# A 512-column product for both parts of the tokens in the input products of four FFNs

## Chip, core and metric

The kernel runs on one core of one Trainium2 chip. The metric is the device time of one execution in microseconds (us). Besides the timed runs there is one execution that was recorded by the hardware profiler; every duration below is from that recording.

The engines are called as the profile calls them: PE (TensorE; PEld is its weight load), DVE (VectorE), ACT (ScalarE), POOL (GpSimd) and SP (SyncE, which here only issues DMAs). Each engine works through its own instructions in program order and waits on semaphores for the others.

## What is computed

A trunk of two layers for 256 tokens of 1024 channels. Each layer has three sublayers, each with a residual and a layer norm: half an FFN (SwiGLU), a mixer (S5 in layer 0, gMLP in layer 1), half an FFN. So there are four FFNs, and each computes

```python
def _swiglu(x, w_in, w_out):
    gate, up = jnp.split(x @ w_in, 2, axis=-1)   # w_in: 1024 x 5632
    return (jax.nn.silu(gate) * up) @ w_out      # w_out: 2816 x 1024

h = _layernorm(DN_ALPHA * h + 0.5 * _swiglu(h, w_in, w_out), ln_g, ln_b)
```

All arrays are float32.

## The kernel before

**Two parts.** PE multiplies in the type float32r. To keep precision, each operand is split into a first part `hi` (the value cast to float32r, on ACT) and a second part `lo` (the value minus `hi`, on DVE). A product is the sum of three: hi x hi, hi x lo and lo x hi.

**The weights** come as a stream of 1 MiB blocks, in the order of their use (class `Stream`). SP issues the load of a block into one of 3 `raw` buffers (line 60); a split makes `hi` on ACT (line 82) and `lo` on DVE (line 83), into a ring of 5 pairs. The load of the block three places on waits until the DVE half of a split has freed its `raw` buffer. `ws.tick()` stands at fixed places in the program: it splits the next block if the ring has room, and then takes one piece of background work from a list. In the first FFN that list is the preparation of the S5 parameters (`prepare_s5`): some DVE work, some copies on ACT, and a long queue of small operations on POOL (lines 592 and 596), which begins with `turn_a`: four transposes on PE, four copies on ACT (lines 648 and 651), and then an exponential on POOL. POOL also makes the reciprocal root `rstd` for every layer norm (lines 203 and 204), behind what stands in its queue.

**The tokens** stand transposed in `xt`, as [128 channels, 2 halves of the tokens, 2 parts, 8 k, 128 tokens].

**An FFN** works in 11 chunks of 256 gate and 256 up columns. The first chunks are computed with tokens on the partitions (`start_in` in the first FFN, chunk 0; `step_in` in the others, chunks 0 and 1). All others, 10 in the first FFN and 9 in each of the three others, go through `chunk_in`: for m (two halves of 128 columns), for g (gate, up), for k (8 steps of 128 channels), the three products of `mm3t` with 256 columns, one for each token, into a PSUM tile [128, 2 g, 256 tokens]. Then `act_t`: silu of the gate from PSUM on ACT (line 368), times the up half from PSUM on DVE (line 369), a cast for the first part on ACT (370) and a difference for the second on DVE (371), into `gt`. Two chunks later `step_out` multiplies `gt` with the rows of `w_out` (512 columns, lines 183 to 185, tile `acc`). `close` does the last three chunks' output products and the norm, and it begins the next sublayer's transposes of `h`.

**Buffers.** PSUM pool `mm` has 4 buffers of one bank; the input products' tiles (`ips`) and the transposes' tiles (`tps`, `aps`) take turns in them. `sgg` (silu and product) has 2 buffers, in which the first FFN's two column tiles of chunk 0 stand before chunk 1 begins; the transposes `tps` of `finish_g`, which come after the products of chunk 1's first half, are the last to read those. `gt` has 7 buffers, and POOL's tables `tb` take turns in them.

Of the kernel before, what the change touches and what calls it, by code (L numbers as in the profile page):

```python
# [9 lines left out]
F32 = mybir.dt.float32  # L10
# [3 lines left out]
ALU = mybir.AluOpType  # L14
# [27 lines left out]
class Stream:  # L42
    """Weights in the order of their use: 1 MiB blocks that are loaded ahead and split into two float32r parts."""
# [41 lines left out]
    def split_pieces(self, n):  # L85
        """Begins to split a block; the returned function splits one of n pieces of it."""
        nc = self.nc
        raw, hi, lo = self.next_block()

        def piece(p):  # L90
            s = slice(p * SUB // n, (p + 1) * SUB // n)
            nc.scalar.copy(hi[:, s], raw[:, s])  # L92
            nc.vector.tensor_tensor(lo[:, s], raw[:, s], hi[:, s].bitcast(F32), op=ALU.subtract)

        return piece

    def split_slowly(self):
        """Splits a block but for the second parts, which the returned two pieces of work make."""
        nc = self.nc
        raw, hi, lo = self.next_block()  # L100
        nc.scalar.copy(hi, raw)

        def rest(p):
            s = slice(p, p + SUB // 2)
            nc.vector.tensor_tensor(lo[:, s], raw[:, s], hi[:, s].bitcast(F32), op=ALU.subtract)
            if p and self.n_loaded < len(self.specs):
                self.load()

        return [lambda p=p: rest(p) for p in (0, SUB // 2)]
# [6 lines left out]
    def tick(self, n=1, pieces=1, eng=None):  # L116
        """Splits up to n more blocks, as far as the ring has room; then a piece of the work that nothing waits for."""
        while n and self.n_split < len(self.specs) and self.n_split - self.n_done < N_SPLIT:
            self.split(pieces, eng)
            self.fill()  # L120
            n -= 1
        if self.background:
            self.background.pop(0)()
# [13 lines left out]
def hybrid(ctx: ExitStack, tc: tile.TileContext, a: dict, out: bass.AP, subs=SUBS):  # L137
# [26 lines left out]
    def transpose_split(src, hi, lo, n, perm=False):  # L164
        """Transposes n 128-column blocks of src [128 tokens, n*128] into hi/lo [128, n, 128]; perm: tokens ordered
        by (token % 4, token // 4)."""
        ps = mm_p.tile([P, 512], F32, tag="mm", name="tps")
        for j in range(n):
            nc.tensor.transpose(ps[:, j * P:(j + 1) * P], src[:, j * P:(j + 1) * P], ident)
        v = ps[:, :n * P].rearrange("p (n t) -> p n t", n=n)  # L170
        if perm:
            v = v.rearrange("p n (k t) -> p n t k", t=T)
            hi, lo = (x.rearrange("p n (t k) -> p n t k", t=T) for x in (hi, lo))
        nc.scalar.copy(hi, v)
        nc.vector.tensor_tensor(lo, v, hi.bitcast(F32), op=ALU.subtract)
# [11 lines left out]
    def mm3t(ps, wh, wl, k, start, stop):  # L187
        """The product with the columns of w on the partitions, for all tokens."""
# [3 lines left out]
        nc.tensor.matmul(ps, wl, xh, start=False, stop=stop)  # L192

# [21 lines left out]
    def layernorm(t, acc, gb, hscale, eps):  # L215
        """h <- LN(hscale*h + acc)"""
# [10 lines left out]
    def add_cols(w, col, width):  # L227
        """Two blocks with the columns [col, col + width) of w: [128, 4 k, width] each."""
# [6 lines left out]
    def add_rows(w, row):  # L235
        """One block with 256 rows of w: [128, 2 k, 1024]."""
# [16 lines left out]
    def close(li, si, acc, blocks, mm, gb, hscale, eps, last):  # L253
        """The last blocks of a sublayer's output product, then its norm: half 0, then half 1 beside the next sublayer."""
# [20 lines left out]
    def plan_ffn(li, fi, fine):  # L275
# [3 lines left out]
        def add_in(c):  # L279
            """Two blocks: [128, 4 k, (gate, up), 256]."""  # L280
# [26 lines left out]
    def ffn(ids, li, si, first, last):  # L307
# [39 lines left out]
        def chunk_in(c):  # L347
            """A chunk for all tokens, the chunk's columns on the partitions."""
            for m in range(2):
                ps = mm_p.tile([P, 2, SEQ], F32, tag="mm", name="ips")  # L350
                for g in range(2):
                    for k in range(KD):
                        wh, wl = ws.get(ids["in"][c][k // 4])
                        s = slice(512 * (k % 4) + FC * g + P * m, 512 * (k % 4) + FC * g + P * m + P)
                        mm3t(ps[:, g], wh[:, s], wl[:, s], k, k == 0, k == KD - 1)
                    if (m, g) == (1, 1):
                        done(ids["in"][c])
                    if g:
                        act_t(c, m, ps)
# [4 lines left out]
        def act_t(c, m, ps):  # L364
            sgg = g_p.tile([P, 2, SEQ], F32, tag="sgg", name="sgg")
            sg, g = sgg[:, 0], sgg[:, 1]
            x = new_gt(c, m)
            nc.scalar.activation(sg, ps[:, 0], AF.Silu)  # L368
            nc.vector.tensor_tensor(g, ps[:, 1], sg, op=ALU.mult)  # L369
            nc.scalar.copy(x[:, 0], g)  # L370
            nc.vector.tensor_tensor(x[:, 1], g, x[:, 0].bitcast(F32), op=ALU.subtract)  # L371

        def start_in():
            """The first chunk of the kernel, both halves of the tokens after each piece of its weights."""
# [65 lines left out]
    def close_mixer(ids, li, si, operand, gb, hscale, eps, last):  # L440
        """The output product of a mixer; operand(k, t): the two parts of 128 of its columns, transposed."""
# [18 lines left out]
    def load_gmlp(pool):  # L460
        """The parameters of the gMLP mixer but for its two projections; W_s masked and transposed."""
# [24 lines left out]
    def gmlp(plan, par, pool, li, si, first, last):  # L486
# [20 lines left out]
        def step_u(hd):  # L507
            """u of one head, its channels on the partitions."""
# [19 lines left out]
        def spatial(hd):  # L528
            """The token mixing of two heads and the gate, in place of u."""
# [35 lines left out]
    def load_column(pool, src, name):  # L565
        """[1024] as [128, 8], channel 128 j + p at [p, j]."""
# [10 lines left out]
    def prepare_s5(sm, qp, dram):  # L577
        """Parameters of the S5 mixer in the layouts of its use, as pieces of work for the time of the first FFN.

        State s of pair q is state s % 64 of group 2 q + s // 64. Four tokens make one step:  # L580
        S' = lam^4 S + sum over t of lam^(3-t) B u[4k+t], y[4k+3] = Re(C S'), and for t < 3
        y[4k+t] = Re(C lam^(t+1) S) + sum over i <= t of K(t-i) u[4k+i], K(d) = Re(C lam^d B).
        With lam^4 = m e^(i phi), e^(-i phi k) S is a scan with real factors m.
        """
# [28 lines left out]
        def exp(x, name):  # L613
            """e^x: 2^k of the nearest integer k to x / ln 2, in two factors, times a polynomial in the rest."""
# [101 lines left out]
        def spread():  # L716
            """The factors of B with (token of the step, state % 32) on the partitions."""
# [6 lines left out]
        def seed():  # L724
            """The square of a unit number, brought back to length 1."""
# [15 lines left out]
        def grow(x, level, z):  # L741
            """e^(i phi k) for 2^level <= k < 2^(level+1) from those below; x: (cos, sin), [128, q, k]."""
# [34 lines left out]
        # lam^(3-t) B, zero where a state and a channel are of different groups of a pair; its  # L777
        # rows: (token of the step, channel)
# [30 lines left out]
        # the same B with the states on the partitions, for K  # L809
# [16 lines left out]
        # C lam^d with the states on the partitions, zero where the groups differ  # L826
# [16 lines left out]
        def c_lam(d, j, part, e):  # L843
            """C lam^d from C lam^(d-1), the real part or the imaginary part's negative."""
# [65 lines left out]
    def s5(plan, res, qp, li, si, first, last):  # L910
# [29 lines left out]
        def turn_u():  # L940
            """u of 4 x 128 channels: [channel, (token of the step, step)], half of the steps."""
# [20 lines left out]
        def turned(dst, src, ct):  # L962
            """src times the cosines and src times the sines; src: (real, imaginary)."""
# [76 lines left out]
        def finish(n):  # L1040
            """2 z = y (1 + tanh(x / 2)), its tokens in their order, in two parts."""
# [159 lines left out]
```

## Time and profile before

| | us |
|---|---|
| median of 3 runs | 1044.12 |
| lowest, highest | 1043.42, 1046.18 |
| the profiled execution: its own time, the span from the first instruction to the last | 1044.0 |
| PE busy in it | 964.5 (92%) |
| DVE, ACT, POOL busy | 651.6, 413.1, 302.0 |

The stages as the trace shows them: the first FFN to about 256 us, the S5 mixer to about 385, the second FFN to about 577, the third to about 768, the gMLP mixer to about 855, the fourth FFN to the end.

How to read the lines that follow. A timeline row has: start in us, length in us, engine, source line, operation, what it writes and what it reads, shapes, count (neighbours are merged into one row), and in brackets how long its engine had stood idle and which instruction ended that. A row of groups has: line, engine, operation, count, busy us in all and the mean of one in ns, idle time before. Products overlap in PE's pipeline, so the length of one is a latency, and the pace is the distance between two starts.

### The profile page before, as it was taken

The page shows a single profiled execution, that of the slowest core. Times are in us where ns is not written, and L with a number is a line of the kernel's source. Part 1 is how long each engine was busy: PE and PEld are TensorE (multiplying, and loading weights), DVE is VectorE, ACT ScalarE, POOL GpSimd, SP SyncE. Part 2 cuts the span into 40 slices and gives each one's busy share as a digit, 9 for nine tenths or more (in the row PEclk, how much of TensorE's full clock was granted, in tenths as well). Part 3 has the DMA queues.
Part 4 walks back from the last instruction along what each step waited for, and adds up shares of the span by engine and source line. Part 5 has one row for each costly group of instructions (what it writes and reads, how often), then busy time and mean ns, then how long its engine had stood idle before and what let it go on. Part 6 is the DMA issues. An engine that isn't in the chain of part 4 may idle for free.

```text
span 1044.0 us, 16750 instructions
## 1 busy us (share of the span) xinstructions
PE 964.5 (92%) x6988; PEld 871.9 (84%) x6988; DVE 651.6 (62%) x726; ACT 413.1 (40%) x467; POOL 302.0 (29%) x461
## 2 busy tenths in 40 slices
PE   7999974577988889999999999999999999999996
PEld 6999963475877678999999799999978979999995
DVE  5659834588489776654536764545388785545444
ACT  5462333232143244453533363534335535443430
POOL 1589999998156421000000400000031030000001
PEclk9999996697998999999999999999999999999999
DMA  9977553385466434746455667465544565546431
GB/s 282 205 216 236 184 150 126 130 298 180 169 216 239 149 127 161 258 147 216 164 200 178 223 209 258 149 215 170 193 162 174 190 209 194 204 160 221 142 122 41
DMA packets 146124, 194.86 MB, mean 187 GB/s; under 512 B 26992, under 2 KB 117184, under 8 KB 146048
## 3 DMA queue, kind: packets, MB, share of 16 engines
q1 hardware_dynamic: 142304, 180.81, 52.7%
q0 software_dynamic: 3456, 12.45, 3.5%
q8 instruction: 55, 0.90, 0.3%
q10 hardware_dynamic: 288, 0.52, 0.1%
q14 instruction: 21, 0.17, 0.0%
HBM read 183.94 MB, written 9.83 MB: 186 GB/s over the span
## 4 chain that ended last, share of the span: by engine, by line
PE 59%; POOL 20%; DVE 10%; issue 4%; ACT 3%; DMA 2%; SPq 1%; POOLq 0%; DVEq 0%; ACTq 0%
PE ips L192 10%; PE ips L191 10%; PE ips L190 10%; PE acc L183 5%; PE acc L184 5%; PE acc L185 5%; POOL rot L972 3%; DVE lo L83 2%; POOL fac L592 2%; POOL t L592 2%; PE ips L185 2%; POOL cl L592 2%; PE ips L183 2%; PE ips L184 2%; POOL tb L592 2%
## 5 line engine op out<-in xcount | busy, mean ns | idle before, releaser
L83 DVE TENSOR_TENSOR lo<-raw,hi 128x2048 fp32r<-128x2048 f32 (+1 forms) x146 | 333.9, 2318 | 85.2 <-ACT hi L82 82.5
L190 PE MATMUL ips<-xt,hi 128*128 128x256 f32 x1184 | 335.3, 283 | 0.0
L191 PE MATMUL ips<-xt,hi 128*128 128x256 f32 x1184 | 335.0, 283 | 0.0
L192 PE MATMUL ips<-xt,lo 128*128 128x256 f32 x1184 | 335.0, 283 | 0.0
L82 ACT CAST hi<-raw 128x2048 fp32r<-128x2048 f32 (+1 forms) x156 | 275.1, 1797 | 62.7 <-PE acc L185 22.1
L190 PEld LDWEIGHTS ips<-xt,hi 128*128 128x128 f32 x1184 | 227.1, 192 | 1.4
L191 PEld LDWEIGHTS ips<-xt,hi 128*128 128x128 f32 x1184 | 227.2, 192 | 1.4
L192 PEld LDWEIGHTS ips<-xt,lo 128*128 128x128 f32 x1184 | 227.1, 192 | 0.0
L203 POOL TENSOR_SCALAR rstd<-mv 128x1 f32<-128x1 f32 x14 | 10.3, 733 | 586.3 <-DVE mv L224 564.4
L183 PE MATMUL acc<-hi,gt 128*128 128x512 f32 x352 | 141.9, 403 | 29.3 <-ACT hi L82 29.3
L184 PE MATMUL acc<-lo,gt 128*128 128x512 f32 x352 | 141.2, 401 | 4.6 <-DVE lo L83 4.6
L185 PE MATMUL acc<-hi,gt 128*128 128x512 f32 x352 | 140.2, 398 | 0.0
L369 DVE TENSOR_TENSOR sgg<-ips,sgg 128x256 f32<-128x256 f32 x74 | 31.1, 420 | 158.8 <-ACT sgg L368 158.8
L368 ACT ACTIVATE sgg<-ips 128x256 f32<-128x256 f32 x74 | 28.4, 383 | 207.9 <-PE ips L192 204.0
L183 PEld LDWEIGHTS acc<-hi,gt 128*128 128x128 f32 x352 | 68.5, 195 | 43.2 <-ACT hi L82 29.7
L370 ACT CAST gt<-sgg 128x256 fp32r<-128x256 f32 x74 | 30.1, 406 | 149.9 <-DVE sgg L369 100.9
L184 PEld LDWEIGHTS acc<-lo,gt 128*128 128x128 f32 x352 | 68.3, 194 | 18.8 <-DVE lo L83 5.9
L185 PEld LDWEIGHTS acc<-hi,gt 128*128 128x128 f32 x352 | 68.1, 193 | 14.7
L371 DVE TENSOR_TENSOR gt<-sgg,gt 128x256 fp32r<-128x256 f32 x74 | 34.1, 461 | 69.9 <-ACT gt L370 69.9
L183 PE MATMUL ips<-hi,xt 128*128 128x512 f32 x112 | 45.9, 410 | 1.7 <-ACT hi L92 1.0
L972 POOL TENSOR_TENSOR rot<-rot 128x256 f32<-128x256 f32 x32 | 35.8, 1137 | 40.1 <-DVE rot L966 39.8
L185 PE MATMUL ips<-hi,xt 128*128 128x512 f32 x112 | 45.0, 402 | 0.1
(250 smaller groups left out, 1275.9 us busy)
## 6 DMA issues: line engine op xcount, KB each, us to landing
raw<-in_ffn_w_in SPq DMA_DIRECT2D x172, 512.0 KB, 5.5
raw<-in_ffn_w_out SPq DMA_DIRECT2D x44, 1024.0 KB, 5.1
raw<-in_g_w_in SPq DMA_DIRECT2D x8, 1024.0 KB, 5.9
rows<-w SPq DMA_DIRECT2D x8, 512.0 KB, 6.0
raw<-in_s_w_in SPq DMA_DIRECT2D x4, 1024.0 KB, 5.5
raw<-in_s_w_glu SPq DMA_DIRECT2D x4, 1024.0 KB, 5.0
w<-rows SPq DMA_DIRECT2D x8, 512.0 KB, 5.8
tc<-tc SPq DMA_DIRECT2D x8, 512.0 KB, 5.1
```

Source lines behind the costliest of these rows:

```text
L82: nc.scalar.copy(hi[:, s], raw[:, s])
L83: eng[p % len(eng)].tensor_tensor(lo[:, s], raw[:, s], hi[:, s].bitcast(F32), op=ALU.subtract)
L183: nc.tensor.matmul(ps, xh, wh, start=start, stop=False)
L184: nc.tensor.matmul(ps, xh, wl, start=False, stop=False)
L185: nc.tensor.matmul(ps, xl, wh, start=False, stop=stop)
L190: nc.tensor.matmul(ps, wh, xh, start=start, stop=False)
L191: nc.tensor.matmul(ps, wh, xl, start=False, stop=False)
L192: nc.tensor.matmul(ps, wl, xh, start=False, stop=stop)
L369: nc.vector.tensor_tensor(g, ps[:, 1], sg, op=ALU.mult)
L371: nc.vector.tensor_tensor(x[:, 1], g, x[:, 0].bitcast(F32), op=ALU.subtract)
L592: e.tensor_tensor(o, x, y, op=op)
L972: G.tensor_tensor(dst[:, j], x, z, op=ops[j])
```

## The change

The three products of one k become two. `mm3t` stays for the gMLP mixer; `chunk_in` calls a new `mm2t`:

```diff
+    def mm2t(ps, wh, wl, k):
+        both = ps.rearrange("p j (t c) -> p j t c", t=2)
+        nc.tensor.matmul(both, wh, xt[:, :, :, k].rearrange("p t j c -> p j t c"), start=k == 0, stop=False)
+        nc.tensor.matmul(ps[:, 0], wl, xt[:, :, 0, k], start=False, stop=k == KD - 1)
...
         def chunk_in(c):
             for m in range(2):
-                ps = mm_p.tile([P, 2, SEQ], F32, tag="mm", name="ips")
+                ps = [mm_p.tile([P, 2, SEQ], F32, tag="mm", name="ips") for _ in range(2)]
+                sgg = g_p.tile([P, 2, SEQ], F32, tag="sgg", name="sgg")
                 for g in range(2):
                     for k in range(KD):
...
-                        mm3t(ps[:, g], wh[:, s], wl[:, s], k, k == 0, k == KD - 1)
+                        mm2t(ps[g], wh[:, s], wl[:, s], k)
                     if (m, g) == (1, 1):
                         done(ids["in"][c])
-                    if g:
-                        act_t(c, m, ps)
+                    nc.scalar.copy(sgg[:, g], ps[g][:, 1])
+                    nc.vector.tensor_tensor(sgg[:, g], sgg[:, g], ps[g][:, 0], op=ALU.add)
+                    if g == 0:
+                        nc.scalar.activation(sgg[:, 0], sgg[:, 0], AF.Silu)
+                    else:
+                        act_t(c, m, sgg)
                     if (m, g) == (0, 1):
                         finish_g()
                     ws.tick()
 
-        def act_t(c, m, ps):
-            sgg = g_p.tile([P, 2, SEQ], F32, tag="sgg", name="sgg")
-            sg, g = sgg[:, 0], sgg[:, 1]
-            x = new_gt(c, m)
-            nc.scalar.activation(sg, ps[:, 0], AF.Silu)
-            nc.vector.tensor_tensor(g, ps[:, 1], sg, op=ALU.mult)
+        def act_t(c, m, sgg):
+            x, g = new_gt(c, m), sgg[:, 1]
+            nc.vector.tensor_tensor(g, g, sgg[:, 0], op=ALU.mult)
             nc.scalar.copy(x[:, 0], g)
             nc.vector.tensor_tensor(x[:, 1], g, x[:, 0].bitcast(F32), op=ALU.subtract)
```

The first part of the weights is multiplied with both parts of the tokens in one product of 512 columns, whose two halves land in the two halves of a PSUM bank; the product of the second part of the weights adds to the first half. Gate and up have a bank each. ACT copies the second half to `sgg`, DVE adds the first half to it. Silu and the product with it then read `sgg`, not PSUM. The rest of the diff removes comments. The lines after the change are numbered higher by 7 in `step_in` and the functions before it, and by 9 from `start_in` on.

PE, the beginning of `chunk_in(1)` in the first FFN (`hi_237` and `lo_238` are the parts of a block of `w_in`, `hi_244` and `lo_245` those of the next): before,

```order
L190 MATMUL ips<-xt,hi_237 128x256
L191 MATMUL ips<-xt,hi_237 128x256
L192 MATMUL ips<-xt,lo_238 128x256
L190 MATMUL ips<-xt,hi_244 128x256
L191 MATMUL ips<-xt,hi_244 128x256
L192 MATMUL ips<-xt,lo_245 128x256
```

and after the change:

```order
L198 MATMUL ips<-xt,hi_237 128x512
L199 MATMUL ips<-xt,lo_238 128x256
L198 MATMUL ips<-xt,hi_244 128x512
L199 MATMUL ips<-xt,lo_245 128x256
```

Each pair of products with the first part of the weights has become one of 512 columns.

ACT in the same place, from the silu of the first FFN's two column tiles to the copies of `turn_a` (`ar`), behind which POOL's queue stands (`hi` from `raw` is a split): before,

```order
L331 ACTIVATE sgg<-ips 128x256 x2
L82 CAST hi_287<-raw_234 128x2048
L368 ACTIVATE sgg<-ips 128x256
L370 CAST gt<-sgg 128x256
L325 CAST gt<-tps 128x128 x4
L82 CAST hi_346<-raw_241 128x2048
L82 CAST hi_385<-raw_248 128x2048
L648 COPY ar<-aps 128x32
```

and after:

```order
L338 ACTIVATE sgg<-ips 128x256 x2
L366 COPY sgg<-ips 128x256
L369 ACTIVATE sgg<-sgg 128x256
L82 CAST hi_284<-raw_234 128x2048
L366 COPY sgg<-ips 128x256
L379 CAST gt<-sgg 128x256
L332 CAST gt<-tps 128x128 x4
L82 CAST hi_335<-raw_241 128x2048
L366 COPY sgg<-ips 128x256
L369 ACTIVATE sgg<-sgg 128x256
L82 CAST hi_371<-raw_248 128x2048
L657 COPY ar<-aps 128x32
```

The copy and the silu of a gate half now stand ahead of the split from `raw_234`, and those of the next gate half between the two splits that stood together. The first copy writes the `sgg` buffer that the transposes `tps` read last.

DVE in the same place (`lo` from `raw` is the DVE half of a split, `cz` a buffer of the S5 preparation): before,

```order
L332 TENSOR_TENSOR sgg<-ips,sgg 128x256 x2
L83 TENSOR_TENSOR lo_288<-raw_234,hi_287 128x2048
L829 MEMSET cz_294 128x1024
L369 TENSOR_TENSOR sgg<-ips,sgg 128x256
L371 TENSOR_TENSOR gt<-sgg,gt 128x256
L326 TENSOR_TENSOR gt<-tps,gt 128x128 x4
L83 TENSOR_TENSOR lo_347<-raw_241,hi_346 128x2048
```

and after:

```order
L339 TENSOR_TENSOR sgg<-ips,sgg 128x256 x2
L367 TENSOR_TENSOR sgg<-sgg,ips 128x256
L83 TENSOR_TENSOR lo_285<-raw_234,hi_284 128x2048
L838 MEMSET cz_291 128x1024
L367 TENSOR_TENSOR sgg<-sgg,ips 128x256
L378 TENSOR_TENSOR sgg<-sgg 128x256
L380 TENSOR_TENSOR gt<-sgg,gt 128x256
L333 TENSOR_TENSOR gt<-tps,gt 128x128 x4
L83 TENSOR_TENSOR lo_336<-raw_241,hi_335 128x2048
```

An addition stands ahead of the DVE half of the first split and another behind the memset, and the product (`L378`) has both its operands in `sgg`.

## Prediction

> **What bounds the kernel now.** I read the page's slices and its chain first.
>
> ```profile
> PE   7999974577988889999999999999999999999996
> ...
> POOL 1589999998156421000000400000031030000001
> ...
> PE 59%; POOL 20%; DVE 10%; issue 4%; ACT 3%; DMA 2%; SPq 1%; POOLq 0%; DVEq 0%; ACTq 0%
> ```
>
> TensorE (PE) is full from the sixteenth slice on, and POOL is full from the third to the tenth. The chain that ended last is 59% PE and 20% POOL. So the kernel has two regimes, and the table by stretches separates them (columns: stretch, length, busy time and count of PE, PEld, DVE, ACT, POOL, then clock, DMA share, GB/s).
>
> ```profile
> 36.80:250.90 214.10, 173.86 (x1371) 159.23 (x1369) 142.99 (x137) 76.03 (x80) 195.66 (x354) 0.90 0.64 198
> ...
> 592.00:768.00 176.00, 175.71 (x1192) 162.84 (x1191) 93.51 (x89) 76.38 (x83) 4.90 (x7) 1.00 0.61 205
> ```
>
> In an FFN such as the third (second row) PE is busy 175.7 of 176.0 us while DVE and ACT are about half idle: there a shorter PE stream is a shorter kernel. In the first FFN (first row) POOL, which prepares the S5 parameters, is busy 195.7 of 214.1 us while PE has 40 us idle. The timeline shows that this stage ends with POOL:
>
> ```profile
> 36.76 0.35 POOL L596 TENSOR_SCALAR ldt<-ldt 128x32 f32<-128x32 f32 x1 [18.86 <-ACT dg L651]
> ...
> 70.06 0.59 POOL L592 TENSOR_TENSOR mag<-mag,ee 128x32 f32<-128x32 f32 x2 [1.17 <-DVE ee L636]
> ...
> 251.97 0.97 POOL L204 TENSOR_TENSOR rstd<-rstd,mhalf 128x1 f32<-128x1 f32 x1
> ...
> 252.98 5.58 DVE L213 SCALAR_TENSOR_TENSOR h<-r,rstd,bet 128x512 f32<-128x512 f32 x2 [0.47 <-POOL rstd L204]
> ...
> 255.86 1.11 PE L169 MATMUL tps<-ident,h 128*128 128x128 f32 x4 [5.46 <-DVE h L213]
> ```
>
> POOL starts when ACT has copied the parameters (36.76), then stands in one queue to the `rstd` of the first norm at 251.97, which DVE waits for and PE waits for in turn. Only one wait on another engine in that queue matters, 1.17 us at 70. A PE that is faster in the first FFN therefore gains nothing there, and a POOL that starts later ends later.
>
> **PE: the term that gains.** Start to start in the second FFN:
>
> ```profile
> 559.82 0.28 PE L190 MATMUL ips<-xt,hi 128*128 128x256 f32 x1
> ...
> 562.58 0.28 PE L192 MATMUL ips<-xt,lo 128*128 128x256 f32 x1
> ...
> 564.09 0.39 PE L183 MATMUL acc<-hi,gt 128*128 128x512 f32 x1
> ...
> 570.88 0.39 PE L183 MATMUL acc<-hi,gt 128*128 128x512 f32 x1
> ...
> L190 PE MATMUL ips<-xt,hi 128*128 128x256 f32 x1184 | 335.3, 283 | 0.0
> ```
>
> From the first to the second row are 23 steps of 256 columns: 2.76 / 23 = 120.0 ns. From the third to the fourth are 30 steps of 512 columns: 6.79 / 30 = 226.3 ns. (The 283 ns of the group is one product's latency; they overlap, so the pace counts.) Twice 120.0 is 13.7 ns more than 226.3: a product pays that much whatever its width. Per k the change replaces three narrow products (360.0 ns) by a wide and a narrow one (346.3 ns), one weight load fewer. The 1184 k-steps are 32 in each of 37 chunks; 27 chunks lie in FFNs 2 to 4, which PE bounds: 27 x 32 x 13.7 ns = **11.8 us gained**. No row shows a wide product that reads its columns in four runs; the bounds are no saving (0) and 11.8, and I take 11.8, because 256 columns in two runs and 512 in one leave the same 13.7. The other 10 chunks (4.4 us) are in the first FFN and count nothing.
>
> The Trainium skill, "TensorE: Matmul & The Clock Gate", section "Back-to-back issue gap", gives a product N / 2.4 + 2.5 ns; by it the saving would be about 2.5 ns per k and 2.2 us in all. The trace disagrees: 120.0 and 226.3 where the page has 109.2 and 215.8.
>
> **ACT and DVE in FFNs 2 to 4.** Each half-chunk gains two copies (ACT) and two additions (DVE). The nearest rows are `L368` (0.38 us) and `L369` (0.42 us), both quoted below with 256 columns from PSUM; four of each per chunk of about 17 us are 1.6 us, on engines about half idle. The gate's pair is done while PE works on the up half, so it is hidden. The up half's addition is not hidden in a sublayer's last chunk: the weight splits queue behind it on DVE, and the norm behind them.
>
> ```profile
> 566.09 4.49 DVE L83 TENSOR_TENSOR lo<-raw,hi 128x2048 fp32r<-128x2048 f32 x2 [1.40 <-ACT hi L82]
> 570.50 0.68 DVE L221 SCALAR_TENSOR_TENSOR r<-h,acc 128x512 f32<-128x512 f32 x1
> ...
> 576.78 0.39 PE L185 MATMUL acc<-hi,gt 128*128 128x512 f32 x1
> 578.31 0.66 PE L169 MATMUL tps<-ident,h 128*128 128x128 f32 x4 [1.14 <-DVE h L213]
> ```
>
> The norm follows the splits without a break, and PE waits for its `h` (1.14 us). So the added 0.42 and a hand-over, 0.45 us, are late at PE after the second and third FFN: **0.9 us lost**.
>
> PSUM: each gate and each up tile now takes a buffer, so a product waits for the addition of the tile four before it (one chunk, 17 us) instead of two chunks. In FFNs 2 to 4 that addition comes within about 3 us, behind three splits. Nothing is lost.
>
> **The first FFN: the term that loses.** The rows of its start, ACT, then DVE:
>
> ```profile
> 24.05 1.90 ACT L82 CAST hi<-raw 128x2048 fp32r<-128x2048 f32 x1
> ...
> 29.74 0.38 ACT L368 ACTIVATE sgg<-ips 128x256 f32<-128x256 f32 x1 [3.79 <-PE tps L322]
> ...
> 30.61 0.41 ACT L370 CAST gt<-sgg 128x256 fp32r<-128x256 f32 x1 [0.49 <-DVE sgg L369]
> ...
> 32.69 3.73 ACT L82 CAST hi<-raw 128x2048 fp32r<-128x2048 f32 x2
> ...
> 36.53 0.22 ACT L651 COPY dg<-aps 128x16 f32<-128x16 f32 x1
> ...
> 28.46 0.91 DVE L829 MEMSET cz<- 128x1024 f32 x1 [0.16 <-issue]
> ...
> 30.15 0.42 DVE L369 TENSOR_TENSOR sgg<-ips,sgg 128x256 f32<-128x256 f32 x1 [0.78 <-ACT sgg L368]
> ...
> 34.63 4.51 DVE L83 TENSOR_TENSOR lo<-raw,hi 128x2048 fp32r<-128x2048 f32 x2 [1.51 <-ACT hi L82]
> ```
>
> Of chunk 1's first `sgg` the row at 29.74 shows the wait: its buffer is still read by the transposes `tps` behind both column tiles. Now that wait sits on the gate's copy, which stands **ahead** of the split at 24.05. ACT is in order, so that split is held, and with it all that follows. From the same durations: copy, addition, silu 29.7 to 30.95; split 1.9, to 32.85; its DVE half 2.25, to 35.1; the memset, to 36.0; addition and product, to 36.9; the cast and the two transposed tiles, 2.08 as from 30.61 to 32.69, to 39.0; split 1.9 and its DVE half 2.3, to 43.2; addition and silu of the next gate, to 44.05; split 1.9, to 45.9; then the copies that POOL waits for, 46.2. Before, the two splits at 32.69 ran without a break and the copies ended at 36.75. POOL starts **9.5 us later**; of the 1.17 us at 70 it gets about 0.9 back: 8.6. (The DVE step that it waits for there is behind splits whose loads SP issues when an earlier split frees a buffer; those start 7 to 10 us later too, and by the same steps DVE is there at about 78, when POOL is.) PE, held by these splits and by PSUM, is some 5 us late after two chunks, and DVE gets 1.6 us more per chunk (four additions). Both have room:
>
> ```profile
> 167.83 0.41 ACT L370 CAST gt<-sgg 128x256 fp32r<-128x256 f32 x1 [24.80 <-POOL s5t L592]
> ...
> 199.26 0.40 ACT L370 CAST gt<-sgg 128x256 fp32r<-128x256 f32 x1 [14.67 <-POOL s5t L592]
> ```
>
> Twice ACT, and DVE and PE behind it, stand 25 and 15 us for buffers that POOL holds.
>
> The other cost is that POOL stalls beside DVE:
>
> ```profile
> 83.18 0.41 DVE L369 TENSOR_TENSOR sgg<-ips,sgg 128x256 f32<-128x256 f32 x1
> ...
> 84.06 0.43 DVE L371 TENSOR_TENSOR gt<-sgg,gt 128x256 fp32r<-128x256 f32 x1 [0.47 <-ACT gt L370]
> ...
> 89.49 2.33 DVE L83 TENSOR_TENSOR lo<-raw,hi 128x2048 fp32r<-128x2048 f32 x1 [1.34 <-ACT hi L82]
> ...
> 83.33 0.25 POOL L592 TENSOR_TENSOR t<-lr,fac 128x32 f32<-128x32 f32 x1
> ...
> 84.20 0.40 POOL L592 TENSOR_TENSOR t<-lr,fac 128x32 f32<-128x32 f32 x1
> ...
> 89.75 2.18 POOL L592 TENSOR_TENSOR t<-lr,fac 128x32 f32<-128x32 f32 x1
> ```
>
> The same POOL operation takes 0.25 us beside a DVE operation that reads PSUM, 0.40 beside a short one with two SBUF operands, and 2.18 beside a long one. The 40 added additions read PSUM: no cost. The 20 products read PSUM before and two SBUF operands now: 0 to 0.43 us each, I take the row's 0.15: 20 x 0.15 = 3.0 us (ends 0 and 8.6). At the stage's end the longer DVE queue (some 5 us for two chunks) falls into the time in which DVE waits for `rstd`: 0 to 2, I take 0. First FFN: 8.6 + 3.0 = **11.6 us lost**.
>
> **Sum.** The profiled execution's own time is its span, 1044.0, with nothing shown outside it; the runs' median is 1044.12. 1044.0 - 11.8 + 0.9 + 11.6 = 1044.7 us: PE's gain in three FFNs is given back in the first.
>
> **Rivals.**
> - Slower, by POOL's stalls: each of the 20 products holds POOL for its whole 0.43 us, 8.6 instead of 3.0, and the DVE queue adds its 2 at the end: 1044.7 + 5.6 + 2 = 1052.3. The place is the stretch up to 251; it decides above 0.28 us each, where 2.6 us more than my 3.0 pass the bound of 0.3%. For it: 2.18 beside the long split. Against it: 0.40 beside the short operation. The Trainium skill, "SBUF — State Buffer", section "SBUF: two separate sides", has this rule: a DVE operation with two SBUF inputs takes the port pair shared with GpSimd exclusively, for the whole instruction. The trace agrees for the split, not for the short one. Chance 0.22.
> - Faster: the late start doesn't reach the end of the first FFN, because POOL has room that I don't see. Fully absorbed it is 1044.7 - 11.6 = 1033.1; half, 1038.9. For it: POOL's busy time contains stalls beside DVE, and these may fall elsewhere. Against it: it never waited over 1.3 us after 36.8. Chance 0.22.
> - The wide product brings no pace, or the four runs cost their own 13.7 ns: 1044.7 + 11.8 = 1056.5. By the page's gap it would be 1054.3. Against it: the rows of PE. Chance 0.08.
>
> **How the numbers follow.** What I forecast, no change, has 0.48. A measurement here tells about 0.3% (3.1 us) from nothing: same is 1041 to 1047, 0.48; slower 0.22 + 0.08 = 0.30; faster 0.22. The range, 1035 to 1053, takes in most of both sides and leaves out a full absorption and the pace that fails. The likeliest case alone has 1041 to 1047.
>
> **What would show it.** In the changed profile: wide products 226 and narrow 120 ns apart, FFNs 2 to 4 shorter by about 11 us together; POOL's first `ldt` at about 46 instead of 36.8; `rstd` of the first norm at about 263; ACT idle from 24 to 29.7 before the gate's copy. If `rstd` comes by 255, the second rival is right; if the start is 46 and `rstd` past 268, the first; if the wide step is over 235 ns, the third.

## The result, and the profile after

The changed kernel takes 1056.55 us (median of 4 runs, 1055.74 to 1057.87) against 1045.15 us (1043.42 to 1047.8): ratio 1.0111, interval 1.0091 to 1.0132. It is **slower by 11.4 us**, outside the predicted range. The profiled execution's span is 1054.5 us, 10.5 above the span before; the run that it belongs to took 1056.29 us.

From the page of the changed kernel, the slices of POOL and the chain that ended last:

```profile
POOL 1289999998426613000000400000021030000001
...
PE 56%; POOL 20%; DVE 13%; issue 5%; ACT 3%; DMA 2%; SPq 1%; POOLq 0%; DVEq 0%; ACTq 0%
```

POOL's second slice has fallen from 5 to 2 tenths and its eleventh has risen from 1 to 4, so it starts later and ends later, and DVE has 13% of the chain instead of 10%. Where the 10.5 us are is read from the table by stretches, one row for each sublayer but the gMLP's, whose 73.4 us did not change. A sublayer ends here where the first transposes `tps` of the next begin; the gMLP mixer's end by that mark is 843.31, while the norm of the second half of its tokens, about 855, comes 12 us later. (Lines up to 192, such as `L169`, have the same numbers in both kernels.) Columns as before: stretch, length, busy time and count of PE, PEld, DVE, ACT, POOL, then clock, DMA share, GB/s. Before:

```profile
255.86:386.18 130.32, 115.11 (x1253) 97.16 (x1253) 98.63 (x170) 41.37 (x56) 54.90 (x50) 0.91 0.51 178
386.18:578.31 192.13, 190.71 (x1249) 174.66 (x1249) 107.61 (x104) 82.07 (x88) 9.22 (x8) 0.99 0.56 186
578.31:769.84 191.53, 190.09 (x1256) 174.34 (x1257) 107.53 (x104) 81.64 (x89) 12.71 (x14) 1.00 0.60 201
843.31:1044.00 200.69, 191.15 (x1258) 175.15 (x1256) 108.04 (x111) 76.35 (x84) 9.35 (x10) 0.99 0.47 158
```

After:

```profile
273.01:401.21 128.20, 112.97 (x1253) 96.72 (x1253) 98.53 (x170) 41.55 (x56) 54.92 (x50) 0.92 0.53 180
401.21:592.05 190.84, 189.00 (x961) 159.34 (x961) 122.03 (x140) 95.38 (x124) 9.22 (x8) 0.99 0.56 188
592.05:782.21 190.16, 188.25 (x969) 158.91 (x969) 121.95 (x140) 94.94 (x125) 12.72 (x14) 1.00 0.60 202
855.62:1054.50 198.88, 189.39 (x970) 159.70 (x968) 122.34 (x147) 89.64 (x120) 9.32 (x10) 0.99 0.47 159
```

The first FFN ends at 273.01 instead of 255.86, **17.15 us later**. S5 is 2.1 us shorter; its instructions are the same, and its clock is 0.92 instead of 0.91, which fits part of it. The second to fourth FFN are 1.29, 1.37 and 1.81 us shorter, 4.5 together: PE's busy time there falls by 5.3, its idle time rises by 0.8. 17.15 - 2.1 - 4.5 is the 10.5. So both sides of the prediction's sum came out worse: the loss is 17 instead of 11.6, the gain 4.5 instead of 10.9.

The first FFN in the timeline of the changed kernel, POOL's queue and then PE:

```profile
46.11 2.17 POOL L605 TENSOR_SCALAR ldt<-ldt 128x32 f32<-128x32 f32 x1 [27.99 <-ACT dg L660]
...
79.43 0.58 POOL L601 TENSOR_TENSOR mag<-mag,ee 128x32 f32<-128x32 f32 x2
...
260.52 0.61 POOL L882 DMA_DIRECT2D kd<-k  x1 [2.20 <-ACT k L880]
261.15 1.93 POOL L601 TENSOR_TENSOR t<-cl,li 128x1024 f32<-128x1024 f32 x1
...
268.22 0.74 POOL L210 TENSOR_SCALAR rstd<-mv 128x1 f32<-128x1 f32 x1 [5.14 <-DVE mv L231]
...
269.05 0.96 POOL L211 TENSOR_TENSOR rstd<-rstd,mhalf 128x1 f32<-128x1 f32 x1
...
273.01 1.09 PE L169 MATMUL tps<-ident,h 128*128 128x128 f32 x4 [6.35 <-DVE h L220]
```

The last operations of POOL's own queue in the timeline of before:

```profile
248.73 0.60 POOL L873 DMA_DIRECT2D kd<-k  x1
249.36 1.93 POOL L592 TENSOR_TENSOR t<-cl,li 128x1024 f32<-128x1024 f32 x1
```

Step by step against before: `ldt` 9.35 us later, `mag` 9.37, the end of POOL's own queue (261.15 + 1.93 = 263.08, against 251.29 in the same way) 11.8, the last `rstd` row 17.1. The last step is new: POOL now **waits 5.14 us for DVE's `mv`**, for which it did not wait before. That is the term which the prediction took as 0. The 2.4 us between `mag` and the end of the queue are mostly a wait too: the DMA `kd` waits 2.20 us for ACT's copy `k`, which stands behind a weight split in ACT's queue, and did not wait before. POOL's busy time on this way is the same, 168.83 us against 168.85.

DVE in the last chunk of the first FFN, before and then after (here with three operations of POOL), from the timelines:

```profile
230.42 0.41 DVE L369 TENSOR_TENSOR sgg<-ips,sgg 128x256 f32<-128x256 f32 x1
...
233.35 1.69 DVE L371 TENSOR_TENSOR gt<-sgg,gt 128x256 fp32r<-128x256 f32 x1 [0.47 <-ACT gt L370]
...
245.78 0.21 DVE L224 BATCH_NORM_AGGREGATE mv<-bst 128x2 f32<-128x12 f32 x1
```

```profile
243.26 4.29 POOL L601 TENSOR_TENSOR cl<-cl,t 128x1024 f32<-128x1024 f32 x1
245.25 0.41 DVE L367 TENSOR_TENSOR sgg<-sgg,ips 128x256 f32<-128x256 f32 x1
...
246.86 0.97 DVE L378 TENSOR_TENSOR sgg<-sgg 128x256 f32<-128x256 f32 x1
248.35 4.55 DVE L380 TENSOR_TENSOR gt<-sgg,gt 128x256 fp32r<-128x256 f32 x1 [0.52 <-ACT gt L379]
248.80 1.93 POOL L601 TENSOR_TENSOR cl<-cl,lr 128x1024 f32<-128x1024 f32 x1
250.68 1.92 POOL L601 TENSOR_TENSOR t<-cl,li 128x1024 f32<-128x1024 f32 x1
...
255.90 2.72 DVE L380 TENSOR_TENSOR gt<-sgg,gt 128x256 fp32r<-128x256 f32 x1 [0.47 <-ACT gt L379]
...
267.92 0.21 DVE L231 BATCH_NORM_AGGREGATE mv<-bst 128x2 f32<-128x12 f32 x1
```

From its first operation to the end of its last difference (`L371`, `L380`) the chunk takes DVE 4.6 us before (230.42 to 235.04) and 13.4 after (245.25 to 258.62). It has four operations more, with their hand-overs to ACT, and its operations with two SBUF operands are stretched, up to 4.55 us where 0.42 is usual: that one ends at 252.90, just behind the two POOL operations that lie beside it, which run on without a stretch. `mv` moved by 22.1 us: 11.8 of these POOL moved too, 5.3 were room (245.99 to 251.25 before), and 5 are left.

PE in the second FFN, after; wide (`L198`) and narrow (`L199`) products take turns, and from the first of these rows to the second are 12 such pairs:

```profile
519.94 0.40 PE L198 MATMUL ips<-xt,hi 128*128 128x512 f32 x1
...
524.18 0.40 PE L198 MATMUL ips<-xt,hi 128*128 128x512 f32 x1
```

4.24 / 12 = 353.3 ns per pair, not 346.3. Over 864 pairs the gain on 360.0 is 5.8 us instead of 11.8.

### The profile page after: what moved, and what is told of

It is laid out like the page before. It is cut to its first block, busy times and chain, and to the rows that moved or that the text cites. A ratio compares the mean times of both kernels' runs of the same rounds, so it can differ in the third digit from the quotient of the medians.

```text
span 1054.5 us, 14683 instructions
## 1 busy us (share of the span) xinstructions
PE 958.4 (91%) x5804; PEld 808.9 (77%) x5804; DVE 712.4 (68%) x874; ACT 466.4 (44%) x615; POOL 303.1 (29%) x461
## 4 chain that ended last, share of the span: by engine, by line
PE 56%; POOL 20%; DVE 13%; issue 5%; ACT 3%; DMA 2%; SPq 1%; POOLq 0%; DVEq 0%; ACTq 0%
PE ips L198 19%; PE ips L199 10%; PE acc L183 5%; PE acc L185 5%; PE acc L184 5%; DVE lo L83 4%; POOL rot L981 3%; POOL fac L601 2%; ACT hi L82 2%; POOL tb L601 2%; DVE h L220 2%; DVE rot L987 2%; PE ips L185 1%; POOL fac L730 1%; PE ips L183 1%
## 5 line engine op out<-in xcount | busy, mean ns | idle before, releaser
L198 PE MATMUL ips<-xt,hi 128*128 128x512 f32 x1184 | 423.6, 401 | 11.2 <-DVE sgg L367 9.4
L199 PE MATMUL ips<-xt,lo 128*128 128x256 f32 x1184 | 333.9, 282 | 0.9 <-DVE lo L83 0.9
L198 PEld LDWEIGHTS ips<-xt,hi 128*128 128x128 f32 x1184 | 224.2, 189 | 68.5 <-DVE sgg L367 12.1
L199 PEld LDWEIGHTS ips<-xt,lo 128*128 128x128 f32 x1184 | 225.4, 190 | 2.5 <-DVE lo L83 1.2
L367 DVE TENSOR_TENSOR sgg<-sgg,ips 128x256 f32<-128x256 f32 x148 | 61.6, 416 | 112.7 <-ACT sgg L366 112.6
L369 ACT ACTIVATE sgg<-sgg 128x256 f32<-128x256 f32 x74 | 31.0, 419 | 136.5 <-DVE sgg L367 136.5
L366 ACT COPY sgg<-ips 128x256 f32<-128x256 f32 x148 | 54.8, 370 | 81.5 <-PE ips L199 74.5
L380 DVE TENSOR_TENSOR gt<-sgg,gt 128x256 fp32r<-128x256 f32 x74 | 40.1, 542 | 63.0 <-ACT gt L379 63.0
L184 PE MATMUL ips<-lo,xt 128*128 128x512 f32 x112 | 44.3, 396 | 0.0
```

Of the source, the lines that this page charges most:

```text
L184: nc.tensor.matmul(ps, xh, wl, start=False, stop=False)
L198: nc.tensor.matmul(both, wh, xt[:, :, :, k].rearrange("p t j c -> p j t c"), start=k == 0, stop=False)
L199: nc.tensor.matmul(ps[:, 0], wl, xt[:, :, 0, k], start=False, stop=k == KD - 1)
L366: nc.scalar.copy(sgg[:, g], ps[g][:, 1])
L367: nc.vector.tensor_tensor(sgg[:, g], sgg[:, g], ps[g][:, 0], op=ALU.add)
```

## The experiments

**1 and 2. Where the loss and the gain are.** The old `chunk_in` beside the new one, chosen by the FFN:

```diff
         def chunk_in(c):
+            if first:          # the other kernel: if not first
+                return chunk_old(c)
```

> The change only in the second to fourth FFN; the first FFN has the old products. Theory (all of the loss is made in the first FFN, and the other three gain what PE's pace gives: 864 k-steps at 352.5 instead of 360.0 ns, 6.5 us, less 0.45 at each of two transitions and some smaller gaps, 4.5 by the changed kernel's own marks): about 1039.5 us against 1044, first norm's transposes at about 256 us. Rival (the changed FFNs lose too, or the gain depends on what the first FFN leaves behind): 1044 or above.

> The change only in the first FFN; the second to fourth have the old products. Theory: the first norm's transposes come at about 273 us instead of 256 as in the changed kernel, S5 gives some 2 us of the 17 back, and the run takes about 1059 us (15 above the kernel before). Rival (the late end of the first FFN comes from weights that are loaded or split for later stages, or from noise in one profile): below 1052.

Measured: the change in the second to fourth FFN alone 1039.46 us (before 1043.56), ratio 0.9952 (0.9937 to 0.9968); in the first FFN alone 1061.23 us, ratio 1.0164 (1.0149 to 1.0179). The timelines have the end of the first FFN, first kernel and then second:

```profile
253.96 1.12 PE L169 MATMUL tps<-ident,h 128*128 128x128 f32 x4 [5.28 <-DVE h L220]
```

```profile
272.10 1.09 PE L169 MATMUL tps<-ident,h 128*128 128x128 f32 x4 [6.32 <-DVE h L220]
```

The whole loss is made in the first FFN, the gain of some 4 us in the others, and the two add up to within some 2 us (13.6 us of loss, against 11.4 for the whole change). Both expectations held (the second by 2 us too low: 17.7 us are lost, no part of the 16.2 at the end of the first FFN is given back).

**3. The buffer on the gate's copy.** The first chunk of the kernel takes its `sgg` tiles from the tag `r`, empty until the norm:

```diff
-            sgg = g_p.tile([P, 2, FC], F32, tag="sgg", name="sgg")
+            sgg = (ln_p if first and c == 0 else g_p).tile([P, 2, FC], F32, tag="r" if first and c == 0 else "sgg", name="sgg", bufs=2)
```

> The whole change, but chunk 0 of the first FFN puts its two gated tiles in two buffers that stand empty until the first norm, so that chunk 1's sums need not wait for the transposes that read them. Theory (the wait for that buffer, on the gate's copy ahead of a weight split in ACT's queue, is what starts POOL late): POOL's first ldt at 37 to 39 us instead of 46, first norm's transposes some 7 to 9 us earlier than the changed kernel's 273, the run at 1048 to 1050 instead of 1056.5. Rival (the copy waits for the gate's product as much as for the buffer, or POOL's queue is bound by something later): ldt at 44 or later, or the end of the first FFN unchanged, the run at 1055 or above.

Measured: 1054.93 us, ratio 1.0096 (1.0077 to 1.0116). **A miss**: the wait for the transposes is gone, but POOL starts only 3.6 us earlier.

```profile
25.99 0.37 ACT L366 COPY sgg<-ips 128x256 f32<-128x256 f32 x1 [1.89 <-PE ips L199]
...
33.24 0.41 ACT L379 CAST gt<-sgg 128x256 fp32r<-128x256 f32 x1 [3.91 <-DVE sgg L378]
...
42.47 2.17 POOL L605 TENSOR_SCALAR ldt<-ldt 128x32 f32<-128x32 f32 x1 [10.92 <-ACT dg L660]
```

The copy now stands at 25.99 instead of 29.63, and behind it ACT still waits 3.91 us for a product that stands behind a weight split in DVE's queue. So the buffer is 3.6 of the 9.35 us of the late start; the rest was taken to be the order of the gate's work and the splits, which the next kernel tests.

**4. The gate's work behind the split again.**

```diff
-                    nc.scalar.copy(sgg[:, g], ps[g][:, 1])
-                    nc.vector.tensor_tensor(sgg[:, g], sgg[:, g], ps[g][:, 0], op=ALU.add)
-                    if g == 0:
-                        nc.scalar.activation(sgg[:, 0], sgg[:, 0], AF.Silu)
-                    else:
-                        act_t(c, m, sgg)
+                    for q in range(2 if g else 0):
+                        nc.scalar.copy(sgg[:, q], ps[q][:, 1])
+                        nc.vector.tensor_tensor(sgg[:, q], sgg[:, q], ps[q][:, 0], op=ALU.add)
+                    if g:
+                        nc.scalar.activation(sgg[:, 0], sgg[:, 0], AF.Silu)
+                        act_t(c, m, sgg)
```

> The whole change, but the gate's copy, addition and silu are issued after the up half, together with the up's, so that the weight split stands ahead of them on ACT and DVE as it did before the change. Theory (the gate's work ahead of the split, with its two hand-overs between ACT and DVE, is what starts POOL late; the buffer was only the 3.6 us that the spare buffer gave back): POOL's first ldt at 37 to 39 us instead of 46, the first norm's transposes at 264 to 266 instead of 273, the run at 1048 to 1050 (S5 may take 2 us of it back). Rival (ACT's and DVE's added operations themselves delay POOL, in whatever order they stand): ldt at 42 or later, the run at 1054 or above.

Measured: 1049.79 us (before 1043.34), ratio 1.0063 (1.0047 to 1.0080).

```profile
36.44 0.35 POOL L605 TENSOR_SCALAR ldt<-ldt 128x32 f32<-128x32 f32 x1 [19.06 <-ACT dg L660]
...
258.71 0.74 POOL L210 TENSOR_SCALAR rstd<-mv 128x1 f32<-128x1 f32 x1 [5.14 <-DVE mv L231]
...
263.50 1.09 PE L169 MATMUL tps<-ident,h 128*128 128x128 f32 x4 [5.98 <-DVE h L220]
```

POOL starts as before the change, and the stage ends 9.5 us earlier than in the changed kernel. The late start is the **order**: the added operations are all still there. The 5.14 us for `mv` stay, word for word, so they are not the late start handed on. (The run's median is 6.8 us below that of the changed kernel; against the kernel before of its own set of runs the loss has fallen from 11.4 to 6.5. That is less than 9.5: in the profiled executions the second to fourth FFN are 1.7 us longer than in the changed kernel, S5 0.4.)

**5 and 6. The end of the stage.** One kernel writes the sums to PSUM, so that the product reads one SBUF operand instead of two:

```diff
-                    nc.vector.tensor_tensor(sgg[:, g], sgg[:, g], ps[g][:, 0], op=ALU.add)
+                    nc.vector.tensor_tensor(ps[g][:, 0], sgg[:, g], ps[g][:, 0], op=ALU.add)
...
-            nc.vector.tensor_tensor(g, g, sgg[:, 0], op=ALU.mult)
+            nc.vector.tensor_tensor(g, ps[:, 0], sgg[:, 0], op=ALU.mult)
```

(the silu reads `ps[0][:, 0]` too). The other has the old products in the first FFN's chunks 9 and 10, by `if first and c >= 9` in the place of experiment 1.

> The whole change, but the sums are written back to PSUM, so that the product reads PSUM and one SBUF operand as it did before the change, instead of two SBUF operands. Theory (a DVE operation with two SBUF operands and POOL's operations hold each other up: POOL by 2.4 us between mag and the last t of its queue, DVE in the products of chunks 9 and 10, 0.97 to 2.88 us instead of 0.42): POOL's stretch from mag to the last t is 179.3 us as before instead of 181.7, the products take 0.4 us throughout, the first norm's transposes come at 267 to 270 instead of 273, the run at 1051 to 1054. Rival (the end of the stage is late by the number of operations in DVE's queue, not by what they read): both unchanged, 1056.

> The whole change but for the last two chunks of the first FFN (9 and 10), which have the old products. Theory (at the end of the first FFN the added operations of these chunks, and their stretching beside POOL's 128x1024 operations, are what makes POOL and PE wait for the norm): POOL's wait for mv falls from 5.14 us to under 1.5, the first norm's transposes come at 268 instead of 273, POOL's first ldt stays at 45 to 46, the run at 1051 to 1052. Rival (the lateness at the end is only the late start, handed on): wait and end unchanged, 1056.

Measured: sums in PSUM 1049.92 us, ratio 1.0064 (1.0047 to 1.0082); old chunks 9 and 10 1050.76 us, ratio 1.0074 (1.0057 to 1.0091). Timelines, the first kernel's last chunk (DVE, and the POOL row beside it), then its POOL queue:

```profile
244.39 0.42 DVE L378 TENSOR_TENSOR sgg<-ips,sgg 128x256 f32<-128x256 f32 x1
245.33 0.43 DVE L380 TENSOR_TENSOR gt<-sgg,gt 128x256 fp32r<-128x256 f32 x1 [0.52 <-ACT gt L379]
245.39 0.94 POOL L865 DMA_DIRECT2D tc<-cl  x1 [0.30 <-POOL cl L601]
```

```profile
79.06 0.58 POOL L601 TENSOR_TENSOR mag<-mag,ee 128x32 f32<-128x32 f32 x2
...
257.20 3.35 POOL L601 TENSOR_TENSOR t<-cl,li 128x1024 f32<-128x1024 f32 x1
...
261.76 0.74 POOL L210 TENSOR_SCALAR rstd<-mv 128x1 f32<-128x1 f32 x1 [1.20 <-DVE mv L231]
...
266.55 0.63 PE L169 MATMUL tps<-ident,h 128*128 128x128 f32 x4 [3.51 <-DVE h L220]
```

The second kernel's:

```profile
45.26 2.17 POOL L631 TENSOR_SCALAR ldt<-ldt 128x32 f32<-128x32 f32 x1 [27.64 <-ACT dg L686]
...
262.85 0.64 POOL L210 TENSOR_SCALAR rstd<-mv 128x1 f32<-128x1 f32 x1
...
267.06 1.11 PE L169 MATMUL tps<-ident,h 128*128 128x128 f32 x4 [5.15 <-DVE h L220]
```

With the sums in PSUM no operation is saved, yet the products take 0.42 us again, POOL's way from `mag` to the end of its queue is 260.55 - 79.06 = 181.5 us (183.65 in the changed kernel, 181.23 before), and the wait for `mv` is 1.20 us. On this way POOL is busy 166.60 us instead of 168.83, its wait for ACT's `k` is gone, and a wait of 2.5 us for DVE's `den` has come. So 2.2 us of POOL's stalls and 3.9 of the 5.1 us at the end came from **what the product reads**, at the end in the main through what follows it: the product is no longer held (0.42 instead of 0.97), the `L380` behind it falls into the pause in which POOL issues a DMA, and takes 0.43 us, where in the changed kernel it comes half a microsecond into that pause, meets POOL's next two operations and takes 4.55. With the old products in two chunks, the waits for `mv` and for `k` are gone altogether, though POOL starts only 0.85 us earlier than in the changed kernel: the end term is made in these two chunks. POOL is busy 171.73 us there from `mag` (78.55) to the end of its queue (262.88), 2.9 more than before: its stalls did grow in the eight other chunks, and in the changed kernel the last two took as much back: there it is DVE that is held.

**7 and 8. PE's pace.** The tokens laid so that a wide product reads one run of columns:

```diff
-    xt = xt_p.tile([P, 2, 2, KD, P], F32R, name="xt")
+    xt = xt_p.tile([P, KD, 2, 2, P], F32R, name="xt").rearrange("p k j t c -> p t j k c")
```

and, with the change in the second to fourth FFN alone, another order of the products:

```diff
                     for k in range(KD):
                         wh, wl = ws.get(ids["in"][c][k // 4])
                         s = slice(512 * (k % 4) + FC * g + P * m, 512 * (k % 4) + FC * g + P * m + P)
-                        mm2t(ps[g], wh[:, s], wl[:, s], k)
+                        mm1w(ps[g], wh[:, s], k)           # the wide product of mm2t
+                    for k in range(KD):
+                        wh, wl = ws.get(ids["in"][c][k // 4])
+                        s = slice(512 * (k % 4) + FC * g + P * m, 512 * (k % 4) + FC * g + P * m + P)
+                        nc.tensor.matmul(ps[g][:, 0], wl[:, s], xt[:, :, 0, k], start=False, stop=k == KD - 1)
```

> The whole change, but the transposed tokens lie so that the 512 columns of a wide product, and the 256 of a narrow one, are one run in memory instead of four and two. Theory (the four runs cost the wide product its 9 ns): wide 226 ns and narrow 120 apart, 346 ns per k instead of 352.5, some 5 us shorter than the changed kernel: 1051.5 us. Rival (the cost comes from wide and narrow products taking turns, or from the weight loads between them): the pair stays at 352 ns and the run at 1056.5.

> The change only in the second to fourth FFN, and there the eight wide products of a column tile go first, then its eight narrow ones. Theory (wide and narrow products in turn cost what the layout of the columns did not: 6 us of 11.8): a wide product 226 ns after another, a narrow one 120, 346 ns a pair, each of these FFNs 1.8 us shorter than with products in turn, the run at 1034 us against 1039.5. Rival (a wide product of this kind takes 235 ns wherever it stands): the pair at 352 or above, 1039.5.

Measured: one run of columns 1055.91 us, ratio 1.0118 (1.0101 to 1.0135), as the changed kernel. Twelve pairs of it, timeline:

```profile
518.73 0.40 PE L198 MATMUL ips<-xt,hi 128*128 128x512 f32 x1
...
522.97 0.40 PE L198 MATMUL ips<-xt,hi 128*128 128x512 f32 x1
```

4.24 us again, 353.3 ns a pair: **the four runs cost nothing**. Wide products first: **1034.2 us, ratio 0.9915 (0.9896 to 0.9933)**, the fastest kernel here. Its timeline merges equal neighbours, and its table by stretches has the second FFN:

```profile
518.04 2.00 PE L196 MATMUL ips<-xt,hi 128*128 128x512 f32 x8
519.88 1.11 PE L372 MATMUL ips<-xt,lo 128*128 128x256 f32 x8
520.83 2.00 PE L196 MATMUL ips<-xt,hi 128*128 128x512 f32 x8
```

```profile
383.57:572.91 189.34, 187.48 (x960) 159.64 (x961) 121.97 (x140) 94.95 (x124) 9.23 (x8) 0.99 0.57 189
```

Eight wide products take 1.84 us, 230 ns each, and eight narrow ones 0.95, 119 each: 348.8 ns a pair. Taking turns is thus most of what was missing, 4.5 of 7 ns; the expected 346 was not quite reached. PE's busy time in the second FFN is 3.2 us below before, against 1.7 in the changed kernel.

**9. All three edits together,** with the change in every FFN.

> The change in every FFN with the three edits together: the gate's copy, addition and silu after the up half, the sums written back to PSUM, the wide products of a column tile ahead of its narrow ones. Theory (late start, operands of the product, and the turns of wide and narrow are the whole loss): POOL's first ldt at 36 to 37 us, its wait for mv at the stage's end under 2 us, the first norm's transposes at 256 to 258 us as before the change, FFNs 2 to 4 each about 2 to 3 us shorter than before, the run at 1035 to 1038, that is 1 to 4 us above the kernel with the old products in the first FFN. Rival (the added copies and additions cost the first FFN more than these three): transposes at 261 or later, the run at 1041 or above.

Measured: 1042.85 us (10 runs; before 1044.18), ratio 0.9990 (0.9980 to 1.0001); the profiled execution's span is 1039.2 us. Timeline:

```profile
252.26 0.74 POOL L214 TENSOR_SCALAR rstd<-mv 128x1 f32<-128x1 f32 x1 [1.20 <-DVE mv L235]
...
257.07 1.08 PE L169 MATMUL tps<-ident,h 128*128 128x128 f32 x4 [2.21 <-DVE h L224]
```

In the first FFN the accounting closes: 15.9 of the 17.15 us are gone, which is what experiments 4 (9.5) and 5 (6.5) took away each by itself. (Differences under 2 us at this mark say little: with the first FFN unchanged, it stood at 253.96, 254.29, 255.76 and 255.86 us in four kernels.) But the run is 5 us above the upper end of what was expected, and PE's waits in the later stages say why:

```profile
PE ips L196 <- ACT sgg L378: 4.0, 3, 2.2
```

Once in each of the second to fourth FFN a product waits for a PSUM tile (columns: waited for, in total, times, longest); the changed kernel has no such row. The gate's tile is now held until after the up half, and the wide products want the next one earlier. That wait, some 4 of the 5 us, was not in the expectation.

**10. Sixteen wide products in a row,** gate's and up's, then the narrow ones (the second to fourth FFN alone): `for g, wide in [(0, True), (1, True), (0, False), (1, False)]`; the gate's `ws.tick()` moves behind the sixteen.

> The change only in the second to fourth FFN; there the sixteen wide products of gate and up go first, then the eight narrow ones of the gate, then those of the up half. Theory (what is lost at a change from narrow to wide is some 23 ns for each such change, spread over the first five wide products; here half as many changes): each of these FFNs 0.4 us shorter than with eight wide and eight narrow, the run at 1033 us against 1034.2, which a measurement can hardly tell. Rival (PE waits for a PSUM buffer or a weight split that now is needed earlier or freed later): above 1036, with idle time of PE ahead of a wide product.

Measured: 1040.75 us, ratio 0.9973 (0.9960 to 0.9987), 6.5 above experiment 8. The rival held; PE's waits after the first FFN:

```profile
PE ips L366 <- DVE sgg L376: 4.8, 3, 2.0
```

With the gate's work where the change put it, eight in a row (experiment 8) goes without that wait and sixteen does not.

## Why the prediction was wrong

Step by step, as the prediction put it:

- **"At the stage's end the longer DVE queue ... 0 to 2, I take 0": this step failed.** The wait was 5.14 us (now the row of `rstd` at 268.22). The prediction put the longer DVE queue at some 5 us for two chunks, with four additions at 1.6 us per chunk, and let it fall into DVE's wait for `rstd`, which had 5.3 us of room. What the runs showed: the last chunk alone became 8.8 us longer on DVE; besides the additions and their hand-overs, its operations with two SBUF operands stand beside POOL's 128x1024 operations and take 0.97 to 4.55 us instead of 0.42; ACT's copy `k` was late as well and cost POOL 2.20 us. The prediction looked only at what DVE does to POOL, not at what POOL does to DVE. The row `L371` of before with 1.69 us instead of 0.42, in that very place, was there to be read. Old products in two chunks (experiment 6) remove the term, operands in PSUM (5) most of it.
- **"no saving (0) and 11.8, and I take 11.8": this step failed too, by about half.** The 226.3 and 120.0 ns were each measured among products of their own width. In turns, a pair takes 353.3. The prediction named the four runs of columns as the doubt; they cost nothing (7). The order does (8). Why PE is slower when widths take turns, and for some products after a change of width, no view shows; that stays open.
- **8.6 for the late start: right but for the 0.9 that was to come back.** Predicted 9.5 later, measured 9.35. Nothing came back at `mag`: POOL's wait of 1.17 us there is gone, but a new one of 0.3 us for `ee` has come and POOL is busy 0.85 us longer on the way (28.10 against 27.25). The prediction's reason held in the main part, the gate's work ahead of the splits (4); the buffer that it named first is 3.6 of it (3).
- **3.0 for POOL's stalls: the number came out near (2.4) by luck.** POOL's busy time did not grow; the 2.4 are the wait of 2.20 for `k` and smaller ones. The mechanism shows only with the old products in the last two chunks: 2.9 us for 16 products, an estimate of 0.18 each.
- **0.9 at the transitions: right.** PE's idle time rose by 0.42 and 0.47 us in the second and third FFN (length less busy time in the table above).
- **PSUM in FFNs 2 to 4, nothing lost: right** for the change as it is made; in experiments 9 and 10, where a tile is held longer, PE waits for one.

The sum, term by term, from 1044.7: the first FFN lost 17.15 instead of 11.6 (+5.5), the other three gained 4.5 instead of 10.9 (+6.4), and S5 was 2.1 shorter instead of unchanged: 1054.5, the measured span. The prediction's own signs pointed to two rivals at once: `rstd` past 268 was given in the main to the stalls of POOL, which were not the cause (168.83 us busy against 168.85), and a wide step over 235 ns to a change that brings no pace, which is half true.

The Trainium skill, "SBUF — State Buffer", section "SBUF: two separate sides", gives the shared port pair for a whole instruction, where that of DVE has two SBUF inputs, to whichever of the two engines starts first. The trace agrees, and in both directions. In the prediction's own two rows POOL's operation ends 0.11 us after DVE's, beside the split (91.93 against 91.82) and beside the short product (84.60 against 84.49). The second cost little because DVE's operation is short and POOL's began 0.14 us into it, not because POOL was not held; so the prediction's "not for the short one" misread it. The other way round, the product at 246.86 began during POOL's `cl` and ends 0.28 us after it (247.83 against 247.55), and so does the 1.69 us row of before (235.04, against 234.76 for POOL's `cl`). Two rows do not fit so simply: `L380` at 248.35 and at 255.90 began 0.45 and 0.49 us ahead of POOL's next operation, while POOL was issuing a DMA, and were held all the same; why is open. The prediction used the rule in one direction only.

## What to carry to other kernels

An operation that becomes cheaper on one engine is paid for where its by-products are queued: put the added copies and sums behind the work that others wait for, not ahead of it. Ask of a stretched row not only which engine it delays but which engine delays it, and look for it at the point where the slack is smallest. A pace that was measured among equal products must not be used for a sequence of mixed ones; keep equal widths together, as far as PSUM has tiles for it, and apply a change only in the stages whose bound it moves (1034.2 us with both, 1039.46 with the second alone, against 1056.55).

## What the runs showed of the hardware that was not expected

- Wide and narrow products in turns: 353.3 ns a pair; eight and eight: 348.8; the sum of the paces of long rows of equals: 346.3. The layout of the columns, four runs or one, made no difference to the first of these.
- A DVE operation of 256 columns with two SBUF operands that began during an operation of POOL ended 0.28 us after it, and an operation of POOL that began during such a one of DVE ended 0.11 us after that, in the rows compared above. The longest took 4.55 us beside two operations of POOL on 128x1024, which themselves took no longer for it (1.93 and 1.92 us); the product of the same chunk took 0.97 us with two SBUF operands and 0.42 with one of them in PSUM.
- S5 took 130.3 us at a clock of 0.91 and 127.8 at 0.94 (255.76 to 383.57 in experiment 8), with the same instructions: the length of this stage goes with the clock, and some 2 us of difference between two spans need not come from the change. No run sets the clock by itself.
